# A two-layer attention encoder: the rotary table in a buffer of its own, the shared key moved ahead of the norms of the latents, and the modulation dot products moved behind it

## The chip, the cores and the metric

The kernel runs on one core of one Trainium2 chip. The time is the device time of one execution in microseconds (us); three executions of the kernel before were timed.

## What is computed

The model has two layers over 1024 tokens of width 1024. A vector `c` modulates each layer: `mod = silu(c) @ ada_w[i] + ada_b[i]` gives a shift, a scale and a gate of 1024 numbers each. Layer 0 mixes two kinds of attention, layer 1 is differential attention.

```python
c_act = jax.nn.silu(c)
for i in range(DEPTH):
    mod = c_act @ ada_w[i] + ada_b[i]
    shift, scale, gate = jnp.split(mod, 3, axis=-1)
    h = rms_norm(x, norm_g[i]) * (1.0 + scale[:, None, :]) + shift[:, None, :]
    ...
    x = x + gate[:, None, :] * out
...
# layer 0
cq, ckv, kr, q_sb, k_sb, v_sb, z = jnp.split(h @ w_in, cuts, axis=-1)
q = (rms_norm(cq, q_norm_g) @ w_uq).reshape(B, S, MLA_HEADS, MLA_NOPE + MLA_ROPE)
q = jnp.concatenate([q[..., :MLA_NOPE], rope(q[..., MLA_NOPE:], pos)], axis=-1)
kv = (rms_norm(ckv, kv_norm_g) @ w_ukv).reshape(B, S, MLA_HEADS, MLA_NOPE + MLA_V)
k_rope = jnp.broadcast_to(rope(kr[:, :, None, :], pos), (B, S, MLA_HEADS, MLA_ROPE))
```

What the change touches: `cq` and `ckv` are the latents, whose norms are needed as one number for each token; `kr` is the one rotated key that all heads share; `rope` needs a table of cosines and sines; `z` is a gate on the output of layer 0. The shift and scale of layer 1 and the two gates are not needed until much later in the program.

## The kernel before, in words

All tensors lie with 128 partitions. Every matrix product runs in three passes (high by high, low by high, high by low, `mm3`, lines 172 to 174) over 8 blocks of 128 inputs, so that a block of 128 outputs by 512 tokens, here called a half, is 24 matmuls. Weight blocks come by DMA into `w_st` (two buffers) and are split into `w_hi` (by ScalarE) and `w_lo` (by GpSimd, line 153). Results go to PSUM banks: three banks `sc`, two banks `psd`, two `tr`, one `pv`.

The stage that matters here ends the opening part, called `a0`, whose buffers are shared by tag (`ld` has six buffers of 1 MB, for weight loads `ada_st` and others; the tags `a` and `b` have four each). In program order it does this: the latents for both halves of the tokens; the rotary table `cs` (ten instructions of VectorE on `ar`, then a sine on ScalarE, line 637); `latent_norm` twice (row sums on the matmul engine at line 233, a reciprocal root on VectorE, a transpose at line 208, and `row_out`, which writes the row to DRAM); the norms read back on all partitions as `rqb`, and `te` and `to`, which combine them with the table and go to `tq_d`; the shared key's block (24 matmuls for each of two halves into `sc` banks, evacuated by VectorE at line 697, which multiplies by `cs`), its rotated copy (`krc`, line 718) and its store `krot_d`; and four `z` blocks of two halves each, evacuated by a sigmoid on ScalarE and a product on VectorE (line 250). Between them `more(n)` places pieces of `ada_rest`: 16 loads of 1 MB of modulation weights (`ada_st<-in_ada_r_dram`), each followed by two dot products with the vector `cb` on VectorE (line 522, `dots`). Then the first attention pair begins with its q/k block (`qk_k`, line 153, evacuated from `psd` banks), then its v block, again in `psd` banks.

A scheduler orders the instructions of each engine; each engine then runs its own in that order. SyncE (SP) issues all DMAs in one order, and each waits there for its buffer and its source. `tc.issue_after(x)` keeps an instruction behind `x` where both are on one engine, and nothing else.

The buffer of `cs` is tag `cs`, which has one buffer, and `cb` was put there first:

```python
cb = a0.tile([P, D], F32, name="cb", tag="cs")
...
cs = a0.tile([P, S], F32, name="cs", tag="cs")
```

So the table can't be written until the last dot product has read `cb`.

Of the kernel before, what the change touches and what calls it, by code (L numbers as in the profile page):

```python
# [11 lines left out]
F32 = mybir.dt.float32  # L12
# [4 lines left out]
ALU = mybir.AluOpType  # L17
# [4 lines left out]
P = 128  # L22
D = 1024
S = 1024
# [47 lines left out]
def kernel(ctx, tc, a, out):  # L72
    nc = tc.nc
    mm = nc.tensor.matmul

    def dma(dst, src):
        dst = dst.bitcast(F32) if dst.dtype == F32R else dst
        src = src.bitcast(F32) if src.dtype == F32R else src
        return nc.sync.dma_start(dst, src)
# [10 lines left out]
    def res(name, dt=F32R):  # L90

        return rpool.tile([P, S], dt, name=name, tag="res")
# [24 lines left out]
    krot_d = dram.tile([P, S], F32, name="krot_d")  # L117
# [37 lines left out]
    def split(hi, lo, src, eng_hi="act", eng_lo="vec"):  # L155

        if eng_hi == "act":
            nc.scalar.copy(hi, src)  # L158
        else:
            (nc.vector if eng_hi == "vec" else nc.gpsimd).tensor_copy(hi, src)  # L160
        return sub(eng_lo, lo, src, hi.bitcast(F32))

    def wprep(src, n=1024, eng_hi="act", eng_lo="pool", alloc=None):
        st = wpool.tile([P, 1024], F32, name="w_st", tag="w_st")
        dma(st[:, :n], src)
        alloc = alloc or (lambda name: wpool.tile([P, 1024], F32R, name=name, tag=name))
        hi, lo = alloc("w_hi"), alloc("w_lo")
        split(hi[:, :n], lo[:, :n], st[:, :n], eng_hi, eng_lo)
        return hi[:, :n], lo[:, :n]

    def mm3(ps, sh, sl, mh, ml, start, stop):
        mm(ps, sh, mh, start=start, stop=False)  # L172
        mm(ps, sh, ml, start=False, stop=False)  # L173
        mm(ps, sl, mh, start=False, stop=stop)  # L174

    def dense_fm(w, rhs, evac, bank=None):

        wh, wl = (t.rearrange("p (k c) -> p k c", c=P) for t in w)
        nk = len(rhs)
        for half in range(2):  # L180
            ps = (bank or d_bank)()
            sl = slice(half * 512, half * 512 + 512)
            for k in range(nk):
                mm3(ps, wh[:, k, :], wl[:, k, :], rhs[k][0][:, sl], rhs[k][1][:, sl], k == 0, k == nk - 1)
            evac(ps, half, sl)
# [290 lines left out]
    hT = [(res(f"h0h{k}"), res(f"h0l{k}")) for k in range(KC)]  # L476
    with tc.tile_pool(name="a0", bufs=1, reuse_waits="tile") as a0:
# [10 lines left out]
        def ada_load(k):  # L488
            ada_st[k] = a0.tile([P, 2, D], F32, name="ada_st", tag="ld", bufs=NLD)
            return dma(ada_st[k].rearrange("p i d -> p (i d)"), a["ada_t"][k - 1] if k else a["ada_0"])  # L490

        def wide(name, tag):
            return a0.tile([P, S], F32, name=name, tag=tag, bufs=4)
# [23 lines left out]
        def dots(st):  # L517

            m = a0.tile([P, 2], F32, name="adm", tag="adm", bufs=4)
            for n in range(2):  # L520
                junk = a0.tile([P, D], F32, name="junkd", tag="junkd")
                nc.vector.tensor_tensor_reduce(junk, st[:, n, :], cb, op0=ALU.mult, op1=ALU.add, scale=1.0, scalar=0.0,
                                               accum_out=m[:, n:n + 1])
            return m
# [8 lines left out]
        def x_mod(g, k, xts, lo):  # L533

            tr = t_bank()
            for j in range(4):
                nc.tensor.transpose(tr[:, j * P:(j + 1) * P], xts[j][:, k * P:(k + 1) * P], identf)
            hf = a0.tile([P, 512], F32, name="hf", tag="hf", bufs=3)
            sl = slice(g * 512, g * 512 + 512)
            nc.scalar.activation(hf, tr, AF.Identity, scale=gsc[0][:, k:k + 1], bias=modc[0][:, k:k + 1])  # L540
            hi = nc.scalar.copy(hT[k][0][:, sl], hf)
            return sub(lo, hT[k][1][:, sl], hf, hT[k][0][:, sl].bitcast(F32)), hi
# [38 lines left out]
        for k in range(KC):  # L581
            if k + 1 < KC:
                known = ada_block(k + 1)
                _, done = x_mod(0, k + 1, x0, "vec")
                if k + 4 < KC:
                    held = ada_load(k + 4)
# [22 lines left out]
        for k in range(KC):  # L609
            ready, _ = x_mod(1, k, x1, "vec")  # L610
# [8 lines left out]
        with tc.issue_after(ready.ins):  # L619

            pos_i = a0.tile([P, 1], I32, name="pos_i")
            dma(pos_i, a["pos"].to_broadcast([P, 1]))
            pos_f = a0.tile([P, 1], F32, name="pos_f")
            nc.vector.tensor_copy(pos_f, pos_i)
            ar = a0.tile([P, S], F32, name="ar", tag="ld", bufs=NLD)
            dma(ar, a["arange"].to_broadcast([P, S]))
            cs = a0.tile([P, S], F32, name="cs", tag="cs")
            nred = a0.tile([P, S], F32, name="nred", tag="junkd")
            nc.vector.tensor_scalar(ar, ar, pos_f, cst[:, 0:1], op0=ALU.add, op1=ALU.mult)
            nc.vector.tensor_scalar(nred, ar, 1.0 / (2.0 * math.pi), cst[:, 1:2], op0=ALU.mult, op1=ALU.add)  # L630
            nc.vector.tensor_scalar(nred, nred, 12582912.0, None, op0=ALU.add)
            nc.vector.tensor_scalar(nred, nred, -12582912.0, None, op0=ALU.add)
            for part in _two_pi_parts():
                nc.vector.scalar_tensor_tensor(ar, nred, -part, ar, op0=ALU.mult, op1=ALU.add)
            nc.vector.tensor_scalar(ar, ar, cst[:, 2:3], 3.1415925, op0=ALU.add, op1=ALU.min)
            nc.vector.tensor_scalar(ar, ar, -3.1415925, None, op0=ALU.max)
            nc.scalar.activation(cs, ar, AF.Sin, scale=cst[:, 3:4])


            lamt = a0.tile([P, 4, 64], F32, name="lamt", tag="ld", bufs=NLD)  # L640
            dma(lamt.rearrange("p n d -> p (n d)"), a["lam"].to_broadcast([P, 256]))
            lj = a0.tile([P, 2, 64], F32, name="lj")
            nc.vector.tensor_mul(lj, lamt[:, 0::2, :], lamt[:, 1::2, :])
            le = a0.tile([P, 2], F32, name="le")
            nc.vector.reduce_sum(le, lj, axis=AX.X)
            nc.scalar.activation(le, le, AF.Exp)
            nc.vector.tensor_tensor(neglam, le[:, 1:2], le[:, 0:1], op=ALU.subtract)
            nc.vector.tensor_scalar(neglam, neglam, -LAM_INIT, None, op0=ALU.add)
            nc.vector.tensor_scalar(subgl, subg, 0.5 * (1.0 - LAM_INIT), None, op0=ALU.mult)
# [17 lines left out]
        def ada_rest():  # L667
            bias = adab.rearrange("p (i n) -> p i n", n=8)
            for n in range(2):
                dst, b_ = ((gt, bias[:, 2::3, :]), (modc[1], bias[:, 3:5, :]))[n]  # L670
                dst = dst.rearrange("p (i n) -> p i n", n=8)
                for k in range(KC):
                    st = a0.tile([P, 2, D], F32, name="ada_st", tag="ld", bufs=NLD)
                    dma(st.rearrange("p i d -> p (i d)"), a["ada_r"][n, k])
                    nc.vector.tensor_tensor(dst[:, :, k], dots(st), b_[:, :, k], op=ALU.add)
                    yield k
        rest = ada_rest()

        def more(n):
            with tc.issue_after(ready.ins):  # L680
                for _ in range(n):
                    next(rest, None)

        def latent_norm(b0, n, row_d):
            part = lambda half, b: sqt[half, b // 2][:, b % 2 * 512:b % 2 * 512 + 512]
            for half in range(2):
                for b in range(b0 + 1, b0 + n):
                    nc.gpsimd.tensor_tensor(part(half, b0), part(half, b0), part(half, b), op=ALU.add)
            ss = row_sums(lambda t: part(t // 4, b0)[:, t % 4 * P:t % 4 * P + P], NT, v_bank)
            r = rstd_cols(a0, ss, NT, 1.0 / (n * P), 1e-6, "rl")  # L690
            row_out(a0, r, NT, row_d, v_bank)


        krt = wide("krt", "b")

        def kr_evac(ps, half, sl):
            nc.vector.tensor_mul(krt[:, sl], ps, cs[:, sl])
        latent_norm(0, 3, rq_d)
        latent_norm(3, 2, rkv_d)
        rqb = wide("rqb", "b")  # L700
        dma(rqb, row_bc(rq_d, P))
        more(3)
        te = wide("te", "a")
        nc.vector.tensor_copy(te[0:64], rqb[0:64])
        nc.vector.tensor_mul(te[64:128], rqb[64:128], cs[64:128])
# [2 lines left out]
        nc.vector.tensor_mul(to[0:64], rqb[0:64], cs[0:64])  # L708
        nc.vector.tensor_copy(to[64:128], rqb[64:128])
        dma(tq_d[1], to)  # L710
        with tc.issue_after(held.ins):
            wkr = wprep(a["w0"][21])
        dense_fm(wkr, hT, kr_evac, s_bank)
        more(2)
        krc = wide("krc", "b")
        for qd in range(4):
            o = qd ^ 1
            nc.scalar.copy(krc[32 * qd:32 * qd + 32], krt[32 * o:32 * o + 32])
        nc.gpsimd.tensor_tensor(krt, krt, krc, op=ALU.add)
        dma(krot_d, krt)  # L720
        more(2)

        for h in range(8):
            dma(rel_d[h], rel_r[h:h + 1, :].to_broadcast([24, NREL]))
# [214 lines left out]
    hT = [(res(f"h1h{k}"), res(f"h1l{k}")) for k in range(KC)]  # L939
# [302 lines left out]
```

## Time and profile before

| | |
|---|---|
| median of 3 runs | 1508.33 us (1505.69 to 1512.91) |
| the profiled execution's own time | 1512.19 us |
| its span | 1510.4 us |
| matmul engine (PE) busy | 1394.5 us, 92% |
| VectorE (DVE) busy | 937.2 us, 62% |
| ScalarE (ACT) busy | 679.3 us, 45% |
| GpSimd (POOL) busy | 421.6 us, 28% |

Times in the rows below are from the start of the span. Busy time of the matmul engine is modelled from pipelined starts, so its matmuls overlap: the distance between two starts is what one costs. An idle time in square brackets stands before an instruction, with what ended it.

### The profile page before, as it was taken

The numbers are of one execution on the slowest core, as the hardware profiler recorded it, in microseconds if no ns is written. First come the engines' busy times: TensorE is split into PE (matmuls) and PEld (weight loads), VectorE is DVE, ScalarE is ACT, GpSimd is POOL, SyncE is SP. The second block draws the span as 40 slices with busy tenths as digits, with TensorE's granted clock in tenths as the row PEclk, the third lists the DMA queues.
The fourth block names the chain that finished last, engine by engine and source line by source line (L and its number), as shares of the span: only waits on it lengthen the run. The fifth ranks groups of instructions, "written<-read, shape, count | busy, mean of one in ns | idle before, by whom it ended". The sixth has DMA issues, their size and how long they took to land.

```text
span 1510.4 us, 20851 instructions
## 1 busy us (share of the span) xinstructions
PE 1394.5 (92%) x7264; PEld 1163.6 (77%) x7264; DVE 937.2 (62%) x2137; ACT 679.3 (45%) x1380; POOL 421.6 (28%) x498
## 2 busy tenths in 40 slices
PE   5992999999998899999889899999999999998897
PEld 4771788888886678887667678888888888886686
DVE  5589127677778866576556616665565756557674
ACT  5630234565555654456444424444444535344321
POOL 2030221132325365535332221122221222133100
PEclk9995999999999899999989999999999999998899
DMA  9567331122315055543557132323232324336262
GB/s 373 216 235 308 117 114 50 49 82 58 94 32 221 29 182 176 166 130 102 178 164 242 48 98 63 84 85 105 77 98 63 91 63 114 79 104 179 79 197 95
DMA packets 110072, 190.38 MB, mean 126 GB/s; under 512 B 8784, under 2 KB 70088, under 8 KB 106896
## 3 DMA queue, kind: packets, MB, share of 16 engines
q1 hardware_dynamic: 109968, 189.05, 39.6%
q8 instruction: 58, 0.95, 0.3%
q14 instruction: 46, 0.38, 0.1%
HBM read 131.75 MB, written 39.27 MB: 113 GB/s over the span
## 4 chain that ended last, share of the span: by engine, by line
PE 39%; DMA 5%; DVE 4%; issue 2%; POOL 2%; ACT 1%; SPq 0%; DVEq 0%; POOLq 0%; ACTq 0%
PE psd L172 8%; PE psd L173 8%; PE psd L174 8%; PE sc L293 4%; PE pv L327 4%; PE sc L172 2%; PE sc L173 2%; PE sc L174 2%; DMA rb<-rst_d 1%; DMA qk_k<-qk_a 1%; DMA w_st<-in_wo_dram 1%; PE pv L233 1%; PE tr L309 1%; PE tr L307 1%; PE tr L308 1%
## 5 line engine op out<-in xcount | busy, mean ns | idle before, releaser
L153 POOL TENSOR_TENSOR w_lo<-w_st,w_hi 128x1024 fp32r<-128x1024 f32 (+2 forms) x61 | 145.1, 2381 | 348.3 <-ACT w_hi L158 348.0
L153 DVE TENSOR_TENSOR pt_l<-tr,pt_h 128x512 fp32r<-128x512 f32 (+1 forms) x240 | 148.9, 631 | 111.2 <-ACT pt_h L158 98.3
L158 ACT CAST pt_h<-tr 128x512 fp32r<-128x512 f32 (+1 forms) x240 | 126.1, 546 | 149.5 <-PE tr L309 141.6
L174 PE MATMUL psd<-h1h,w_lo 128*128 128x512 f32 x448 | 177.0, 395 | 0.0
L173 PE MATMUL psd<-h1l,w_hi 128*128 128x512 f32 x448 | 176.2, 393 | 0.0
L172 PE MATMUL psd<-h1h,w_hi 128*128 128x512 f32 x448 | 176.1, 393 | 0.0
L293 PE MATMUL sc<-qk_k,qk_a 128*128 128x512 f32 (+2 forms) x288 | 105.5, 371 | 5.1 <-DMA qk_a<-qk_a 2.8
L172 PE MATMUL psd<-h0h,w_hi 128*128 128x512 f32 x264 | 105.3, 399 | 0.0
L173 PE MATMUL psd<-h0l,w_hi 128*128 128x512 f32 x264 | 104.6, 396 | 0.0
L174 PE MATMUL psd<-h0h,w_lo 128*128 128x512 f32 x264 | 104.3, 395 | 0.0
L293 PE MATMUL sc<-qk_k,qk_b 128*128 128x512 f32 (+2 forms) x288 | 99.3, 351 | 0.0
L327 PE MATMUL pv<-pt_l,vt 128*128 128x256 f32 x320 | 91.3, 310 | 8.4 <-DVE pt_l L153 7.4
L1057 DVE CUSTOM_DVE_ANT_0 g<-sc,tz 128x512 f32<-128x512 f32 (+3 forms) x128 | 72.1, 585 | 40.8 <-PE sc L293 34.1
L173 PEld LDWEIGHTS psd<-h1l,w_hi 128*128 128x128 f32 x448 | 84.3, 188 | 16.9
L174 PEld LDWEIGHTS psd<-h1h,w_lo 128*128 128x128 f32 x448 | 84.2, 188 | 16.1
L172 PEld LDWEIGHTS psd<-h1h,w_hi 128*128 128x128 f32 x448 | 84.2, 188 | 16.1
L158 ACT CAST w_hi<-w_st 128x1024 fp32r<-128x1024 f32 x55 | 57.8, 1052 | 85.8 <-PE sc L173 39.7
L327 PE MATMUL pv<-pt_h,vt 128*128 128x256 f32 x320 | 91.6, 301 | 2.9 <-POOL pt_h L313 1.7
L1063 ACT ACTIVATE g<-g,st 128x640 f32<-128x640 f32 (+3 forms) x64 | 63.3, 990 | 67.4 <-DVE st L1062 62.5
L777 DVE TENSOR_TENSOR_SCAN g<-g 128x640 f32<-128x640 f32 (+3 forms) x32 | 68.8, 2149 | 14.7 <-ACT g L774 14.5
L327 PEld LDWEIGHTS pv<-pt_l,vt 128*128 128x128 f32 x320 | 64.1, 200 | 12.0 <-DVE pt_l L153 4.7
L327 PEld LDWEIGHTS pv<-pt_h,vt 128*128 128x128 f32 x320 | 63.7, 199 | 9.5 <-POOL pt_h L313 2.2
(458 smaller groups left out, 3722.9 us busy)
## 6 DMA issues: line engine op xcount, KB each, us to landing
w_st<-in_w_dram SPq DMA_DIRECT2D x43, 512.0 KB
ada_st<-in_ada_r_dram SPq DMA_DIRECT2D x16, 1024.0 KB
w_st<-in_wo_dram SPq DMA_DIRECT2D x16, 512.0 KB
ada_st<-in_ada_t_dram SPq DMA_DIRECT2D x7, 1024.0 KB
yh_d<-yh SPq DMA_DIRECT2D x28, 256.0 KB
yl_d<-yl SPq DMA_DIRECT2D x28, 256.0 KB
w_st<-in_wv_dram SPq DMA_DIRECT2D x12, 512.0 KB
qk_b<-qk_k SPq DMA_DIRECT2D x24, 256.0 KB
```

Of the source, the lines that this page charges most:

```text
L153: return (nc.vector if eng == "vec" else nc.gpsimd).tensor_tensor(out_, x_, y_, op=ALU.subtract)
L158: nc.scalar.copy(hi, src)
L172: mm(ps, sh, mh, start=start, stop=False)
L173: mm(ps, sh, ml, start=False, stop=False)
L174: mm(ps, sl, mh, start=False, stop=stop)
L233: mm(ps[:, t:t + 1], tile_of(t), ones, start=True, stop=True)
L293: mm(ps[:, :nn], st[:, q], mv[:, lo_:lo_ + nn], start=m == 0, stop=not diag and m == len(pairs) - 1)
L307: nc.tensor.transpose(tr[:, P:256], pb[:, (2 * j + 1) * P:(2 * j + 2) * P], identf)
L327: mm(dst, st, tt[w][:, m * 256:m * 256 + 256], start=j == 0 and m == 0 and x == 0, stop=j == n - 1 and m == 1 and x == len(ps_) - 1)
L777: nc.vector.tensor_tensor_scan(ur, ur, ur, 1.0, op0=ALU.mult, op1=ALU.bypass)
L1057: nc.vector.tensor_tensor_reduce(e_[:, sl], ps, tz[:, S - L + sl.start:S - L + sl.stop], op0=ALU.add, op1=ALU.max, scale=1.0, scalar=-3e38 ...
L1063: nc.scalar.activation(e_[:, :L], e_[:, :L], AF.Exp, scale=0.125, bias=st[:, 2 + c:3 + c], accum_out=lst[:, c1:c1 + 1] if c == 0 else st[: ...
```

## The change

The rotary table gets one of the four buffers of tag `b` (and `krt` one of tag `a`), so that it no longer waits for `cb`. The shared key's block comes ahead of the norms of the latents. Of the 16 weight loads of `ada_rest` two stay early, and 14 must be issued behind the store of the rotated key (`turned`); the calls of `more` that stood between the norms and the key are gone.

```diff
-            cs = a0.tile([P, S], F32, name="cs", tag="cs")
+            cs = wide("cs", "b")
...
                 for k in range(KC):
                     st = a0.tile([P, 2, D], F32, name="ada_st", tag="ld", bufs=NLD)
-                    dma(st.rearrange("p i d -> p (i d)"), a["ada_r"][n, k])
-                    nc.vector.tensor_tensor(dst[:, :, k], dots(st), b_[:, :, k], op=ALU.add)
+                    with tc.issue_after((turned if n or k > 1 else held).ins):
+                        dma(st.rearrange("p i d -> p (i d)"), a["ada_r"][n, k])
+                    with tc.issue_after(turned.ins):
+                        nc.vector.tensor_tensor(dst[:, :, k], dots(st), b_[:, :, k], op=ALU.add)
                     yield k
...
         def more(n):
-            with tc.issue_after(ready.ins):
-                for _ in range(n):
-                    next(rest, None)
+            for _ in range(n):
+                next(rest, None)
...
-        krt = wide("krt", "b")
+        krt = wide("krt", "a")
...
+        with tc.issue_after(held.ins):
+            wkr = wprep(a["w0"][21])
+        dense_fm(wkr, hT, kr_evac, s_bank)
         latent_norm(0, 3, rq_d)
         latent_norm(3, 2, rkv_d)
         rqb = wide("rqb", "b")
         dma(rqb, row_bc(rq_d, P))
-        more(3)
...
-        with tc.issue_after(held.ins):
-            wkr = wprep(a["w0"][21])
-        dense_fm(wkr, hT, kr_evac, s_bank)
-        more(2)
...
-        dma(krot_d, krt)
-        more(2)
+        turned = dma(krot_d, krt)
+        more(4)
```

On VectorE, at the key's evacuation (`krt<-sc,cs`, which frees two of the three `sc` banks), the kernel before has this order:

```order
L675 TENSOR_TENSOR modc_121<-adm,smalls 128x2
L522 ISA junkd,adm<-ada_st,cb 128x1024
L522 ISA adm 128x1
L522 ISA junkd,adm<-ada_st,cb 128x1024
L522 ISA adm 128x1
L704 COPY te<-rqb 64x1024
L709 COPY to<-rqb 64x1024
L675 TENSOR_TENSOR modc_121<-adm,smalls 128x2
L705 TENSOR_TENSOR te<-rqb,cs 64x1024
L708 TENSOR_TENSOR to<-rqb,cs 64x1024
L697 TENSOR_TENSOR krt<-sc,cs 128x512 x2
```

The same engine in the changed kernel, at the same evacuation (`lat_l` is the last of the latents, `gt` the gates' column, `rlh` the first step of the norms' root):

```order
L522 ISA junkd,adm<-ada_st,cb 128x1024
L522 ISA adm 128x1
L522 ISA junkd,adm<-ada_st,cb 128x1024
L522 ISA adm 128x1
L605 SCALAR_TENSOR_TENSOR lat_l<-sc,smalls,lat_h 128x512
L677 TENSOR_TENSOR gt<-adm,smalls 128x2
L698 TENSOR_TENSOR krt<-sc,cs 128x512 x2
L191 TENSOR_SCALAR rlh<-pv 128x8
```

The evacuation of the key stood behind the dot products of all 16 loads; now it stands behind those of two, and ahead of the norms, of `te` and of `to`.

Further on VectorE, at the evacuation of the first q/k block (`qk_k<-psd,qk_a`), before:

```order
L697 TENSOR_TENSOR krt<-sc,cs 128x512 x2
L242 TENSOR_SCALAR gsc_123<-modc_121 128x8
L250 TENSOR_TENSOR zb<-zb,sc 128x512
L243 TENSOR_TENSOR gsc_123<-gsc_123,smalls 128x8
L250 TENSOR_TENSOR zb<-zb,sc 128x512 x7
L153 TENSOR_TENSOR qk_k<-psd,qk_a 128x512 x2
```

and in the changed kernel, at the same place:

```order
L677 TENSOR_TENSOR modc_121<-adm,smalls 128x2
L522 ISA junkd,adm<-ada_st,cb 128x1024
L522 ISA adm 128x1
L522 ISA junkd,adm<-ada_st,cb 128x1024
L522 ISA adm 128x1
L677 TENSOR_TENSOR modc_121<-adm,smalls 128x2
L242 TENSOR_SCALAR gsc_123<-modc_121 128x8
L243 TENSOR_TENSOR gsc_123<-gsc_123,smalls 128x8
L153 TENSOR_TENSOR qk_k<-psd,qk_a 128x512 x2
```

Before, only products of `z` blocks stood ahead of it; now the dot products of all the weight loads do.

On the queue of SyncE, behind the row of norms (`rq_d`) and ahead of the first attention's weights, the changed kernel has:

```order
L79 DMA rq_d<-row 8x128
L79 DMA rqb<-rq_d 128x1024
L79 DMA tq_d<-te 128x1024
L79 DMA tq_d<-to 128x1024
L79 DMA krot_d<-krt 128x1024
L79 DMA ada_st<-in_ada_r_dram 128x2048 x2
L79 DMA zs_d<-zb 128x1024
L79 DMA ada_st<-in_ada_r_dram 128x2048 x4
L79 DMA w_st<-in_w_dram 128x1024
L79 DMA ada_st<-in_ada_r_dram 128x2048
L79 DMA rkv_d<-row 8x128
L79 DMA zs_d<-zb 128x1024
```

Before, all 16 `ada_st` loads stood ahead of `rqb`, and `krot_d` followed `tq_d` in the same way. The other seven now follow in the same manner, between two more stores of `z` and three more weight blocks.

## Rows read from the trace of the kernel before

**Rows 1.** The page: busy tenths of the matmul engine in 40 slices of 37.8 us.

```profile
PE   5992999999998899999889899999999999998897
```

**Rows 2.** Waits of the matmul engine, 98 to 220 us: total, times, longest.

```profile
PE sc L172 <- DVE krt L697: 17.9, 1, 17.9
```

**Rows 3.** Timeline of the matmul engine: start, duration, instruction, [idle before <- releaser].

```profile
98.70 0.50 PE L172 MATMUL sc<-h0h,w_hi 128*128 128x512 f32 x1
...
100.66 0.95 PE L233 MATMUL pv<-ones_sq,lsq 128*128 128x1 f32 x8
...
116.83 0.39 PE L174 MATMUL sc<-h0h,w_lo 128*128 128x512 f32 x1
...
153.11 0.80 PE L172 MATMUL sc<-h0h,w_hi 128*128 128x512 f32 x1 [17.90 <-DVE krt L697]
...
154.13 0.63 PE L174 MATMUL sc<-h0h,w_lo 128*128 128x512 f32 x1
154.56 0.63 PE L172 MATMUL sc<-h0h,w_hi 128*128 128x512 f32 x1
...
159.15 0.39 PE L173 MATMUL sc<-h0l,w_hi 128*128 128x512 f32 x1
159.38 0.39 PE L174 MATMUL sc<-h0h,w_lo 128*128 128x512 f32 x1
...
215.37 0.60 PE L268 MATMUL tr<-identf,vs 128*128 128x128 f32 x4
```

**Rows 4.** Timeline of ScalarE: the rotary table, and the swapped copy of the key.

```profile
148.47 1.15 ACT L637 ACTIVATE cs<-ar,smalls 128x1024 f32<-128x1024 f32 x1 [34.48 <-DVE adm L522]
...
153.74 4.20 ACT L718 COPY krc<-krt 32x1024 f32<-32x1024 f32 x4 [2.21 <-DVE gsc L242]
```

**Rows 5.** Timeline of VectorE: dot products, and one instruction that reads PSUM.

```profile
92.08 0.74 DVE L605 SCALAR_TENSOR_TENSOR lat_l<-psd,smalls,lat_h 128x512 fp32r<-128x512 f32 x1
...
104.30 0.16 DVE L675 TENSOR_TENSOR gt<-adm,smalls 128x2 f32<-128x2 f32 x1
...
111.49 1.23 DVE L522 CUSTOM_DVE_ANT_0 junkd<-ada_st,cb 128x1024 f32<-128x1024 f32 x1
...
112.83 3.44 DVE L522 CUSTOM_DVE_ANT_0 junkd<-ada_st,cb 128x1024 f32<-128x1024 f32 x1
...
138.13 1.22 DVE L522 CUSTOM_DVE_ANT_0 junkd<-ada_st,cb 128x1024 f32<-128x1024 f32 x1
...
140.73 1.22 DVE L522 CUSTOM_DVE_ANT_0 junkd<-ada_st,cb 128x1024 f32<-128x1024 f32 x1
```

**Rows 6.** Windows: busy time of each engine, granted clock, DMA share, GB/s.

```profile
110.00:115.00 5.00, 5.00 (x23) 4.13 (x22) 5.00 (x12) 2.34 (x2) 2.23 (x1) 1.00 1.04 436
135.00:140.00 5.00, 0.22 (x1) 0.00 (x0) 4.68 (x10) 0.00 (x0) 0.00 (x0) 0.50 1.01 419
```

**Rows 7.** Queue of SyncE and GpSimd: a row of norms out to DRAM and back.

```profile
988.89 0.30 SPq L79 DMA_DIRECT2D rst_d<-row  x1
...
993.60 1.29 POOL L1089 TENSOR_TENSOR zt<-zt,rb 128x512 f32<-128x512 f32 x1 [2.94 <-DMA rb<-rst_d]
```

**Rows 8.** VectorE by line and form, 98 to 220 us: count, busy, mean ns, idle.

```profile
L250 DVE TENSOR_TENSOR zb<-zb,sc 128x512 f32<-128x512 f32 x8 | 5.5, 687 | 36.7 <-ACT zb L248 36.7
...
L708 DVE TENSOR_TENSOR to<-rqb,cs 64x1024 f32<-64x1024 f32 x1 | 1.2, 1218 | 0.0
...
L709 DVE COPY to<-rqb 64x1024 f32<-64x1024 f32 x1 | 0.7, 691 | 0.0
```

**Rows 9.** Timeline of GpSimd: the low halves of weight blocks.

```profile
87.83 6.59 POOL L153 TENSOR_TENSOR w_lo<-w_st,w_hi 128x1024 fp32r<-128x1024 f32 x2 [22.42 <-ACT w_hi L158]
...
112.77 2.42 POOL L153 TENSOR_TENSOR w_lo<-w_st,w_hi 128x1024 fp32r<-128x1024 f32 x1 [12.74 <-ACT w_hi L158]
```

**Rows 10.** Queue of SyncE: the first and last of the q/k copies.

```profile
206.83 0.54 SPq L79 DMA_DIRECT2D qk_b<-qk_k  x1
...
213.31 0.47 SPq L79 DMA_DIRECT2D qk_a<-qk_a  x1
```

## The prediction

> **What bounds the kernel now.** I read the page first: the matmul engine is busy for 92% of the span, and after the first slice its strip falls to 2 in one place only, the slice from 113 to 151 us [rows 1], so that one hole is worth a look of its own. The waits of that engine in this stretch come next: the longest, 17.9 us, is on the key's evacuation by VectorE [rows 2], and small instructions of the norms break up the rest of the hole. The timeline of the matmul engine gives the hole its edges: the last matmul of the first `z` half starts at 116.83, the first of the second half at 153.11 [rows 3]. The reader is to see that the second is of the same block as the first, and that only a bank was missing. Three `sc` banks exist; two held the two halves of the key, the third the first half of `z`. ScalarE's timeline says why the key was not evacuated: it stood idle for 34 us before the sine that makes `cs`, released by a dot product of VectorE [rows 4]. `cs` shares its one buffer with `cb`, which every dot product reads. So the hole is a buffer's, not an engine's: the matmul engine waits for the table, the table for the last of 16 weight loads of 1 MB.
>
> Inside the hole VectorE and the DMA engines both work without a pause: a pair of dot products takes 2.60 us from start to start (138.13 to 140.73) [rows 5], and the DMA share is full at 419 GB/s [rows 6]. That work isn't removed by the change. It moves, and the question is what it meets.
>
> **The change part by part.**
>
> *Removed.* In the changed order the key is evacuated behind the dots of two loads. Before, these were done at 104.3 [rows 5], and the sine needs none of them now; the key's two halves end at about 105 and 111 (48 matmuls from 98.70 [rows 3]). So the bank for the second half of the first `z` block is free before it is asked for, and the hole closes: 153.11 less 117.06 (the last start plus one step of 0.23) is 36.0 us. Behind the hole the first 12 matmuls also ran at the lower level of the clock, 1.2 GHz, 0.43 us apart where the later ones are 0.23 apart [rows 3]; the granted clock in the hole is 0.50 [rows 6]: 12 x 0.20 = 2.4 us more. Together 38.4.
>
> *Added on the matmul engine's path.* The row sums of the second latent and three transposes ran inside the hole and now stand between matmuls: 16 rows of line 233 at 0.95 us for 8 [rows 3], 1.9, and three transposes at 0.3 (four take 0.60 in the last of [rows 3], so this estimate is generous), 0.9; 2.8 in all. The moved key block costs what it cost. Net 35.6 us. Before, the v block ends at 215.37, and its 48 matmuls take 10.9 (48 x 0.227 [rows 3]), so the first q/k block ended at 204.5. By this sum it ends at 168.9.
>
> *Where the dots go.* The loads may start only behind the store of the key, and that stands on SyncE behind a chain, which I follow in time. The transpose of the norms is 8 matmuls into the second `z` half, 118.9; its copy and the issue of `rq_d`, 119.5. Out to DRAM and back on all partitions took 4.7 us for a row of half the width (988.89 to 993.60 [rows 7]); with 0.6 for the other half 124.8. `te` and `to` are two copies at 0.69 and two products at 1.22 [rows 8], 3.8, done at 128.6. The key's own part (its copy on ScalarE, 4.20 [rows 4], and GpSimd's sum of 2.4, taken as one such instruction [rows 9]) is over by 118.5 (111 + 0.7 + 4.2 + 2.4) and doesn't count. So the key's store issues at 129.0, and the first of 14 loads at 129.3. Ahead of it in the DMA engines are `te`, `to` and the key, 0.52 MB each; from 127.1, with about 1.2 us to start (an estimate from the 4.7 us of two such trips and their 0.26 MB [rows 7]) and 2.6 MB at 0.425 MB/us (between the two rates of [rows 6]), the first load is there at 134.5, say 135.
>
> From there two bounds. *DMA*: 14 loads of 1.05 MB, four `z` stores and four weight blocks of 0.52 MB that stand between them, and the three stores ahead: 20.45 MB, 48.1 us from 128.3, so the last load lands at 176.4 and its dots end at 179.0. *VectorE*: 14 x 2.60 = 36.4; five evacuations of `z` halves that lie between at 0.69 [rows 8], 3.4; two rows of norms and gates, 0.6; and what GpSimd takes. One dot product that began beside a GpSimd split took 3.44 us instead of 1.23, the split 2.42 [rows 5, 9]: 2.2 lost. Four splits fall into this stretch (the last `z` block, two q/k, one v), 8.8. That ends at 184.2. An evacuation that reads PSUM kept its 0.74 in the middle of two such splits [rows 5, 9], so I charge nothing for those.
>
> The Trainium skill, page "SBUF — State Buffer", section "SBUF: two separate sides", says that GpSimd and a VectorE instruction with two SBUF inputs take one shared port pair as an exclusive lock for a whole instruction, the loser fully blocked. By that rule a split costs its full 2.4, four 9.6, and VectorE would end at 185.0; without any such lock it would end at 175.4 and the DMA bound of 179.0 would hold. The row agrees with the rule.
>
> I take VectorE's bound, since the row of 3.44 is this same pair of instructions, and keep 179.0 for the low end. Two small instructions and one evacuation (0.3 + 0.7) later the first q/k half is out of its bank: 185.2, or 180.0.
>
> *The new wait.* The first q/k evacuation now stands behind all dots on VectorE. The v block needs that `psd` bank. The `z` halves themselves don't wait. Each needs the evacuation of the third half back. With 5.45 us a half from 117.1 and the additions above, the matmul engine asks for one at 130 that stands behind `te` and `to` (out at 129.3), and at 147 and 152 for two that stand behind one and two loads (out at 138 and 144). So the matmul engine runs to 168.9 and stands until 185.2: 16.3, plus 2.4 for the low clock again, 18.7. Behind the v block stand the three copies of q and k, issued over 6.5 us before (206.83 to 213.31 [rows 10]), so about 195 against an end of v at 198.5: hidden, with 3 us to spare.
>
> *The other edits.* `krt` in tag `a` and `cs` in tag `b` take buffers whose last readers, the transposes of `x` and the sums of squares, stand ahead of the key's block; nothing. The later gates and modulation are wanted hundreds of us later; nothing. The scheduler also interleaves the following attention differently; the matmul engine is full there, so I give it 0 and 4 us either way.
>
> **Sum.** 35.6 - 18.7 = 16.9 us. Span 1510.4 to 1493.5, the profiled execution's own time 1512.19 to 1495.3; that execution is 3.9 above the median, so the median goes from 1508.33 to 1491.4. Half a per cent, 7.5 us, is about what a measurement here can tell from no change.
>
> **The rivals.**
>
> *A shorter stall.* The DMA bound decides, or the chain to the key's store is quicker. At 180.0 the stall is 11.1 + 2.4 and the gain 22.1: 1486. If the dots end by 168.9 there is none: 35.6, 1473. For it: GpSimd's two splits at 87.83 took 6.59 where two alone take 4.8 [rows 9], so some of the loss may fall on GpSimd, which has time. Against the last: 20.45 MB from 128.3 to 166 would need 540 GB/s, against 436 in [rows 6].
>
> *A longer stall.* Each us by which the store of the key or the stream is late is a us lost. At four fifths of the rate that I took the stream needs 60 us and the last dots end at 191, a gain of 10: 1498; with the store of the key 4 us late too, 195, a gain of 6: 1502. The stores of `z` and the row of norms make such delays possible, since SyncE waits at each. The Trainium skill, "DMA: Bandwidth & Descriptors", section "Where 436 GB/s comes from", holds HBM to about 358 GB/s for one core, by which I estimate 57.1 us for the stream, dots until 188.0 and 1495; the 419 and 436 of [rows 6] contradict it.
>
> *Slower than before.* The queue of SyncE becomes a ring: a load behind a `z` store, the store behind an evacuation, that behind the dots of the load before. If each load ran alone, 1.2 + 2.5 + 2.6 = 6.3 us, 14 end at 217, the v block starts 15 us later than before: 1523. The point that decides is 5.2 us for each load, (202.1 - 129.3) / 14. Against it: six buffers, and six loads issued with one store between them.
>
> *It doesn't do what it says*: `cs` waits for another reader in tag `b`. Then the hole stays, 1508. The earlier tile in that buffer is an `x` tile, long read, so little speaks for it.
>
> **How the numbers follow.** Forecast (1486 to 1498) 0.60; shorter stall (1473 to 1486) 0.22; longer (1498 to 1507) 0.12; slower 0.03; unchanged 0.03. The likeliest is 1491.4. The range 1475 to 1499 holds the forecast, most of the shorter stall and a little of the longer. Faster by over 0.5% (under 1500.8): 0.60 + 0.22 + 0.04 = 0.86. Slower 0.03. Within: 0.11.
>
> **What would show it.** Right: no wait for `krt` in the matmul engine; the sine at about 102; the first late load issued at 129; the `z` blocks without a gap; one wait of 11 to 19 us before the v block, on `qk_k`; dot products of 3.4 us beside splits. Wrong: waits inside the `z` blocks, the DMA share below full between 130 and 175, a start of the loads far from 129, or scores that wait for the copies of q and k.

## The result and the profile after

The changed kernel takes 1493.59 us (median of 4 runs, 1491.70 to 1493.87). The kernel before, with a fourth run, takes 1508.99 us (median, 1505.69 to 1512.91). The ratio is 0.9894, 95% interval 0.9869 to 0.9920: 15.4 us faster. The profiled execution took 1493.56 us, its span is 1491.8 us against 1510.4. The forecast was 1491.4 us.

The page, busy time of the matmul engine and its strip in 40 slices (now of 37.3 us), answers to [rows 1]:

```profile
PE 1386.7 (93%) x7264; PEld 1155.6 (77%) x7264; DVE 950.9 (64%) x2137; ACT 679.3 (46%) x1380; POOL 428.3 (29%) x498
...
PE   5999599999998799998879899999999999997797
```

The slice that read 2 is gone, and the next one reads 5: it runs from 149 to 186 us. The waits of the matmul engine from 98 to 220 us (total, times, longest) answer to [rows 2]:

```profile
PE psd L172 <- DVE qk_k L153: 15.6, 1, 15.6
PE sc L172 <- DVE zb L250: 0.7, 1, 0.7
```

The wait for the key is no longer there, and one new wait has come, for the first q/k evacuation. The timeline of the matmul engine answers to [rows 3]:

```profile
130.24 0.50 PE L172 MATMUL sc<-h0h,w_hi 128*128 128x512 f32 x1 [0.75 <-DVE zb L250]
...
184.56 0.80 PE L172 MATMUL psd<-h0h,w_hi 128*128 128x512 f32 x1 [15.65 <-DVE qk_k L153]
...
198.37 0.60 PE L268 MATMUL tr<-identf,vs 128*128 128x128 f32 x4
...
198.72 0.47 PE L293 MATMUL sc<-qk_k,qk_a 128*128 128x512 f32 x1
```

The reader is to see three things. The `z` half that asks for a bank at 130 loses only 0.75 us. The first q/k block is done at 168.91 (184.56 less 15.65). The scores start right behind the v block, with no wait for the copies of q and k. The transpose of v stands at 198.37; it stood at 215.37 in [rows 3], so the stage ends 17.0 us earlier; 0.57 of these were gained ahead of it (the key's block starts at 98.13, at 98.70 in [rows 3]). The other 1.6 us of the span's 18.6 lie somewhere behind the stage; no run looks for them.

ScalarE has the sine of the table at 101.01, where [rows 4] had it at 148.47:

```profile
101.01 1.16 ACT L637 ACTIVATE cs<-ar,smalls 128x1024 f32<-128x1024 f32 x1
```

VectorE's timeline answers to [rows 5]: the key's second half, the copy of `te`, the first late dot product, two dot products and two small instructions that met a GpSimd split, the first dot product of the last load, and the q/k evacuation.

```profile
110.33 0.69 DVE L698 TENSOR_TENSOR krt<-sc,cs 128x512 f32<-128x512 f32 x1 [5.30 <-PE sc L174]
...
123.98 2.11 DVE L707 COPY te<-rqb 64x1024 f32<-64x1024 f32 x1 [5.09 <-DMA rqb<-rq_d]
...
136.60 1.23 DVE L522 CUSTOM_DVE_ANT_0 junkd<-ada_st,cb 128x1024 f32<-128x1024 f32 x1 [3.24 <-DMA ada_st<-in_ada_r_dram]
...
137.87 3.29 DVE L522 CUSTOM_DVE_ANT_0 junkd<-ada_st,cb 128x1024 f32<-128x1024 f32 x1
...
155.20 2.81 DVE L522 CUSTOM_DVE_ANT_0 junkd<-ada_st,cb 128x1024 f32<-128x1024 f32 x1
...
161.35 1.55 DVE L677 TENSOR_TENSOR modc<-adm,smalls 128x2 f32<-128x2 f32 x1
...
175.77 2.17 DVE L677 TENSOR_TENSOR modc<-adm,smalls 128x2 f32<-128x2 f32 x1
...
180.80 1.23 DVE L522 CUSTOM_DVE_ANT_0 junkd<-ada_st,cb 128x1024 f32<-128x1024 f32 x1 [0.25 <-DMA ada_st<-in_ada_r_dram]
...
183.82 1.28 DVE L153 TENSOR_TENSOR qk_k<-psd,qk_a 128x512 fp32r<-128x512 f32 x2
```

From 136.60 to 183.82 VectorE has no idle time but 0.25 us, and these are for the last load: both bounds of the prediction end at the same place. GpSimd's splits, one beside `te` and the first and last of that stretch, answer to [rows 9], the windows (busy time of each engine, clock, DMA share, GB/s) to [rows 6]:

```profile
123.19 2.35 POOL L153 TENSOR_TENSOR w_lo<-w_st,w_hi 128x1024 fp32r<-128x1024 f32 x1 [5.28 <-ACT w_hi L158]
136.96 3.12 POOL L153 TENSOR_TENSOR w_lo<-w_st,w_hi 128x1024 fp32r<-128x1024 f32 x1 [11.42 <-ACT w_hi L158]
...
174.55 3.37 POOL L153 TENSOR_TENSOR w_lo<-w_st,w_hi 128x1024 fp32r<-128x1024 f32 x1 [11.67 <-ACT w_hi L158]
```

```profile
128.00:130.00 2.00, 1.50 (x7) 0.92 (x5) 1.93 (x4) 0.00 (x0) 0.00 (x0) 1.00 0.63 262
...
130.00:140.00 10.00, 9.76 (x43) 7.99 (x44) 6.45 (x18) 2.14 (x3) 3.04 (x1) 1.00 0.99 349
140.00:150.00 10.00, 10.00 (x45) 8.27 (x45) 9.83 (x19) 1.20 (x2) 0.08 (x1) 1.00 1.02 431
...
170.00:180.00 10.00, 0.00 (x0) 0.00 (x0) 9.79 (x16) 2.02 (x3) 5.21 (x3) 0.67 1.00 397
180.00:190.00 10.00, 5.44 (x13) 4.33 (x14) 4.68 (x12) 0.00 (x0) 0.21 (x4) 0.50 0.53 161
```

From 130 to 180 us the DMA engines are as full as VectorE. The queue of SyncE has the key's store, the first late loads and the copies of q and k ([rows 10] had the first and the last at 206.83 and 213.31):

```profile
129.71 0.38 SPq L79 DMA_DIRECT2D krot_d<-krt  x1
130.15 2.02 SPq L79 DMA_DIRECT2D ada_st<-in_ada_r_dram  x2
...
185.16 0.54 SPq L79 DMA_DIRECT2D qk_b<-qk_k  x1
...
193.61 0.46 SPq L79 DMA_DIRECT2D qk_a<-qk_a  x1
```

### The profile page after: what moved, and what is told of

Read it like the earlier page. It is cut to its first block, busy times and chain, and to the rows that moved or that the text cites. A ratio compares the mean times of both kernels' runs of the same rounds, so it can differ in the third digit from the quotient of the medians.

```text
span 1491.8 us, 20861 instructions
## 1 busy us (share of the span) xinstructions
PE 1386.7 (93%) x7264; PEld 1155.6 (77%) x7264; DVE 950.9 (64%) x2137; ACT 679.3 (46%) x1380; POOL 428.3 (29%) x498
## 4 chain that ended last, share of the span: by engine, by line
PE 39%; DMA 6%; DVE 4%; issue 2%; POOL 2%; ACT 1%; SPq 0%; DVEq 0%; POOLq 0%; ACTq 0%
PE psd L172 7%; PE psd L173 7%; PE psd L174 7%; PE sc L293 4%; PE pv L327 4%; PE sc L172 2%; PE sc L173 2%; PE sc L174 2%; DMA rb<-rst_d 1%; DMA qk_k<-qk_a 1%; DMA w_st<-in_wo_dram 1%; PE pv L233 1%; DMA y_hi<-yh_d 1%; PE tr L307 1%; PE tr L309 1%
## 5 line engine op out<-in xcount | busy, mean ns | idle before, releaser
L153 POOL TENSOR_TENSOR w_lo<-w_st,w_hi 128x1024 fp32r<-128x1024 f32 (+2 forms) x61 | 149.5, 2453 | 369.4 <-ACT w_hi L158 365.5
L172 PE MATMUL psd<-h0h,w_hi 128*128 128x512 f32 x264 | 106.6, 404 | 15.6 <-DVE qk_k L153 15.6
L173 PEld LDWEIGHTS psd<-h1l,w_hi 128*128 128x128 f32 x448 | 84.2, 188 | 16.9
L776 DVE TENSOR_TENSOR_SCAN g<-g 128x640 f32<-128x640 f32 (+3 forms) x32 | 65.8, 2056 | 20.4 <-ACT g L773 20.4
L172 PEld LDWEIGHTS psd<-h0h,w_hi 128*128 128x128 f32 x264 | 50.5, 191 | 25.6 <-DVE qk_k L153 16.1
```

The source lines that it names most:

```text
L153: return (nc.vector if eng == "vec" else nc.gpsimd).tensor_tensor(out_, x_, y_, op=ALU.subtract)
L776: nc.vector.tensor_tensor_scan(ur, ur, ur, 1.0, op0=ALU.mult, op1=ALU.bypass)
```

## The experiments

The theory is that of the prediction: VectorE has 36 us of dot products to do between the norms and the first attention; whoever stands behind them on VectorE waits. The buffer alone doesn't change that, the order does. Rivals: the buffer was the whole hole; the late start of the loads is the whole stall; the DMA stream alone, or VectorE alone, sets its end. Each kernel was timed beside the kernel before on one chip, and ratios are to it.

### The parts of the change

**e1_buffer_alone**: the kernel before with one line.

```diff
-            cs = a0.tile([P, S], F32, name="cs", tag="cs")
+            cs = wide("cs", "b")
```

> The kernel before with one line of the change: the rotary table in a buffer of its own; everything else as before. The theory (the buffer lets the table be early, but where the dot products stand in VectorE's order decides when the banks are freed): the sine moves from 148 to before 110, yet in the order of this kernel the key's evacuation stands behind the dots of about 12 loads and the z products behind those of all 16 and te and to, so the matmul engine still waits about 20 us for the key's evacuation and again for the first z product; the gain is 11 to 14 us, a median of 1495 to 1498. The rival (the buffer was the whole hole, the move of the key and of the loads adds nothing): no wait over 3 us before the z blocks, no wait at the v block either, a gain of about 33 us, 1475.

Measured: 1502.98 us, ratio 0.9962 (0.9947 to 0.9977); span 1500.0. Its waits of the matmul engine, 95 to 222 us:

```profile
PE pv L208 <- DVE rlr L202: 7.8, 2, 6.5
PE sc L172 <- DVE krt L697: 5.3, 1, 5.3
PE sc L172 <- DVE zb L250: 4.9, 1, 4.9
PE pv L233 <- DVE row L210: 3.6, 1, 3.6
```

```profile
137.25 1.28 DVE L697 TENSOR_TENSOR krt<-sc,cs 128x512 f32<-128x512 f32 x2
```

The sine runs at 101.17, yet the key's evacuation only at 137.25, behind the dots of about twelve loads. The rival falls: the buffer alone brings 0.4%. The theory was right on the place and wrong by 5 us on the size: the hole breaks into five waits of 21.6 us together, and I had left out that the small steps of the norms (L202, L210) stand between the dots as well.

**e2_loads_not_held**: the changed kernel, with the late loads free to start early.

```diff
-                    with tc.issue_after((turned if n or k > 1 else held).ins):
+                    with tc.issue_after(held.ins):
```

> The changed kernel, with the 14 late loads free to start as early as the two early ones (not held behind the store of the key). The theory (VectorE has 36 us of dots to do somewhere; held behind the key they meet the v block, not held they meet the z blocks): the z products stand behind all dots on VectorE, the hole comes back at the second z half (about 128 to 151 us), the wait of 15.6 us at the v block goes; 1494 to 1497. The rival (only the late start of the loads costs, earlier loads take the stall away): no wait over 5 us anywhere from 98 to 220, 1475.

Measured: 1504.11 us, 0.9969 (0.9955 to 0.9983). Its waits, 98 to 222 us:

```profile
PE sc L172 <- DVE zb L250: 12.5, 1, 12.5
PE pv L208 <- DVE modc L677: 9.9, 2, 5.7
PE pv L233 <- DVE row L210: 1.6, 1, 1.6
```

The stall at the v block is gone, and 24.0 us of waits stand around the norms and the `z` blocks instead. So most of the gain of the change (10.5 of its 15.4 us by the medians) hangs on holding the loads back, and the rival, that earlier loads would only help, falls. No run holds the loads and leaves the key where it was, so what the key's move adds to the held loads is not shown. The size was missed by 7 us: the dots end at 152.7, `te` and `to` follow, and the second `z` half starts at 157.9 where I had 151.

**e3_loads_behind_read_back** and **e9_early_loads_norms_first**: the changed kernel, the loads held behind the read-back of the norms, 8 us earlier; in e9 the dots also stand behind the second norm's root on VectorE.

```diff
-                    with tc.issue_after((turned if n or k > 1 else held).ins):
+                    with tc.issue_after((back if n or k > 1 else held).ins):
...
-        dma(rqb, row_bc(rq_d, P))
+        back = dma(rqb, row_bc(rq_d, P))
```

```diff
-                    with tc.issue_after(turned.ins):
+                    with tc.issue_after((normed if n or k > 1 else held).ins):
```

> The changed kernel, with the late loads held behind the read-back of the norms (rqb) and not behind the store of the key: the first six loads are issued about 9 us earlier, ahead of the stores of te, to and the key. The theory (the start of the stream sets the end of the dots, both bounds shift with it): the last dots end 6 to 9 us earlier, the wait of 15.6 us at the v block falls to 7 to 10, new waits in the z blocks of at most 3; 1485 to 1489. The rival (VectorE's queue or the copies of q and k behind the v block set the end, the start of the stream does not): the wait stays at 13 to 16 or is replaced in full, 1492 to 1495.

> The changed kernel with the late loads held behind the read-back only, as in e3_loads_behind_read_back, but with the dot products kept behind the reciprocal root of the second norm on VectorE, where they had been mixed into it. The theory (after the norms VectorE alone needs 46 to 47 us for the dots and what lies among them, wherever the stream starts): no wait at the second norm's transpose, the first late dot at 133 to 134 instead of 136.6, the evacuation of the first q/k block at 179 to 182 instead of 183.9, the waits of the matmul engine in the stage 12 to 16 in all; 1488 to 1492. The rival (the start of the DMA stream sets the end, which is 8 us earlier here): the evacuation at 175 to 177, 1484 to 1487.

Measured: e3 1499.83 us, 0.9934 (0.9911 to 0.9957); e9 1494.32 us, 0.9929 (0.9905 to 0.9953). Waits of e3 and VectorE's one long idle time in it:

```profile
PE psd L172 <- DVE qk_k L153: 6.8, 1, 6.8
PE pv L208 <- DVE rlr L202: 5.9, 1, 5.9
PE sc L172 <- DVE zb L250: 2.1, 2, 1.3
```

```profile
160.01 0.69 DVE L250 TENSOR_TENSOR zb<-zb,sc 128x512 f32<-128x512 f32 x1 [5.83 <-ACT zb L248]
```

Waits of e9:

```profile
PE sc L172 <- DVE zb L252: 7.6, 2, 6.9
PE psd L172 <- DVE qk_k L153: 6.8, 1, 6.8
```

The wait at the v block fell to 6.8, about as expected of e3, but the time did not follow. The dots start at 131.5 and 134.0 instead of 136.6, and the first q/k evacuation still comes at 186.5 and 186.2 (183.82 in the changed kernel, whose stage starts 1.2 to 1.4 us sooner). With the loads early, their dots fill VectorE while the `z` blocks run: the matmul engine waits for a bank, then the next sigmoid is late, and VectorE, whose next instruction needs it, stands idle for 5.83 us (3.97 in e9). In e9 14.4 us of waits are left, as expected, in two places instead of one. Two holes also cost the slower start twice: in e3 twelve steps of the matmul engine behind the first (150.37 to 155.66) and thirteen behind the second (187.24 to 192.95) take 0.44 us each, where the changed kernel has thirteen such steps in all. My 1485 to 1489 for e3 was wrong by 11 us. In e9 the theory's time was 2 us too early (6 by the ratio, since the kernel before took 1505.25 there) and its evacuation 4; from its first dot to that evacuation VectorE needed 52.2 us and not 46 to 47. The rival's evacuation was 9 us too early: an earlier stream buys nothing here.

### What sets the length of the stall

**e6_no_mod1_loads**: eight of the 14 late loads and their dots left out.

```diff
+                if n == 1:
+                    nc.vector.tensor_copy(dst, b_)
+                    return
```

> The changed kernel without the 8 loads and 16 dot products of layer 1's shift and scale, which are replaced by their bias (that part of the modulation is left out). The theory: the dots that are left end by about 157 us, before the first q/k block is done at 169; the wait of 15.6 us at the v block and the low clock behind it (2.4) go, at most 3 us of them coming back as a wait for the copies of q and k; 1473 to 1479. The rival (the stall is caused by something else that stands in front of the evacuation): a wait of over 8 us stays there, 1485 or more.

Measured: 1472.66 us, 0.9757 (0.9738 to 0.9776). These waits are left:

```profile
PE sc L293 <- DMA qk_a<-qk_a: 0.9, 1, 0.9
PE sc L172 <- DVE zb L250: 0.8, 1, 0.8
```

The stall comes from these loads and their dots together; this run takes both away and can't say which. The time falls by 20.9 us (1493.59 less 1472.66; ratios 0.9894 less 0.9757 give 20.7). In the trace, from the start of the key's block (99.56) to the transpose of v (181.25), the stage is 18.6 us shorter than in the changed kernel (98.13 to 198.37), which is the stall and its slower start as counted, 15.65 and 2.8. The other 2.3 us lie outside the stage or in the spread of the runs.

**e4_half_dots** and **e5_half_bytes** take half off one bound and leave the other.

```diff
+                        m = dots(st) if n == 0 and k < 2 else dots(st, (0,))
```

```diff
+                            dma(st[:, 0, :], a["ada_r"][n, k][:, 0:D])
```

> The changed kernel with one of the two dot products of each late load (the other half of the modulation behind the key's store is left out), all bytes still loaded. The theory (two bounds of nearly one length, the DMA stream and VectorE, so taking off one gains little): the stream still runs at 0.42 MB/us, the last load lands at 176 to 179, the wait at the v block falls from 15.6 to 9 to 13; 1488 to 1492. The rival (VectorE alone set the end): the dots end near 165, no wait over 3 us at the v block, 1473 to 1478.

> The changed kernel with half the bytes in each of the 14 late loads, both dot products reading that half (half of the weights behind the key's store are left out). The theory (VectorE's own work is 14 x 2.60 for the dots, 3.4 for the z products, 0.6 for rows and about 7 lost to GpSimd's splits, 47.4 in all): first dot at 133 to 135, the dots end at 180.5 to 182.5, the wait at the v block is 13 to 15; 1490 to 1493. The rival (the DMA stream alone set the end): 13 MB are there by 163, the wait falls under 4, 1473 to 1480.

Measured: e4 1488.31 us, 0.9882 (0.9854 to 0.9910); e5 1491.40 us, 0.9894 (0.9870 to 0.9918). In e4, the wait of the matmul engine and the last load's dot on VectorE:

```profile
PE psd L172 <- DVE qk_k L153: 14.5, 1, 14.5
```

```profile
180.84 1.23 DVE L522 CUSTOM_DVE_ANT_0 junkd<-ada_st,cb 128x1024 f32<-128x1024 f32 x1 [2.54 <-DMA ada_st<-in_ada_r_dram]
```

In e5, the wait, the first late dot, and the window of 160 to 170 us:

```profile
PE psd L172 <- DVE qk_k L153: 15.4, 1, 15.4
```

```profile
138.95 3.01 DVE L522 CUSTOM_DVE_ANT_0 junkd<-ada_st,cb 128x1024 f32<-128x1024 f32 x1 [4.05 <-DMA ada_st<-in_ada_r_dram]
```

```profile
160.00:170.00 10.00, 9.70 (x44) 8.06 (x45) 9.86 (x19) 0.82 (x2) 3.23 (x1) 1.00 0.76 270
```

Both rivals fall. With half the dots VectorE waits for the DMA at 12 of the 14 loads, and the last load is there at 180.84, as in the changed kernel (180.80): the stream alone takes that long. With half the bytes the DMA engines have room (share 0.76) and VectorE has none: from its first dot to the q/k evacuation it takes 47.2 us (138.95 to 186.16), as in the changed kernel (136.60 to 183.82). Two bounds of one length: halving either takes 0.2 to 1.2 us off the wait of 15.6, and two traces of the changed kernel alone differ by 0.8 (16.4 in **after_beside_e8** below). The times came out as expected, the places did not quite: in e4 the last load was to land by 179 and the wait to fall to 9 to 13; in e5, whose stage begins 1.5 us later, the first dot was due by 135 and the end of the last by 182.5 (it ends at 185.7). Both sums took a stream that starts at full rate; in e5 even a first load of half the bytes was not there sooner (7.3 us after its issue, 6.4 in the changed kernel).

### A version without the new wait

**e7_qk_off_vector** lets ScalarE copy the first q/k block out and GpSimd subtract; **e8_qk_off_vector_ordered** also keeps the next block's split behind that on both engines, and the next `z` weights behind the copies of q and k on SyncE. From the edit of e8:

```diff
+            if tmp is not None:
+                nc.scalar.copy(tmp[:, sl], ps)
+                hi = nc.scalar.copy(a_t[:, sl], tmp[:, sl])
+                copied[:] = [hi, sub("pool", k_t[:, sl], tmp[:, sl], a_t[:, sl].bitcast(F32))]
...
+                with tc.issue_after(copied[0].ins), tc.issue_after(copied[1].ins):
+                    w_next = wprep(a["w0"][2 * pr + 1])
...
+    with tc.issue_after(copied[2].ins):
+        dma(rkv, row_bc(rkv_d, P))
```

> The changed kernel; the first q/k block alone is copied out of its banks by ScalarE and split there and on GpSimd, so that its evacuation no longer stands behind the dots on VectorE; the copies of q and k go ahead of two loads for later on SyncE. Nothing is left out. The theory (the wait at the v block is nothing but the place of that evacuation behind the dots): no wait on the q/k evacuation, the v block starts at about 169; a new wait of 4 to 8 us behind it, since the attention's buffers lie where the loads lay and are free when the dots end, at about 186 with two more GpSimd splits beside them; 1480 to 1487. The rival (the whole wait comes back at the attention's buffers or at the copies of q and k): 1490 to 1495.

> The kernel of e7_qk_off_vector, where ScalarE's copy of the first q/k block stood behind the split of the second q/k block's weights (which waited for its DMA until 174), and GpSimd's subtraction behind that split too. Here the split of those weights is kept behind the q/k block on both engines, and the weights of the z block of the first pair behind the copies of q and k on SyncE. Nothing is left out. The theory (with the evacuation behind nothing but its own block the v block needs no wait; what is left is the copies of q and k beside the stream, and the end of the dots): the wait of 6.0 us at the v block goes, the first copy issues at 172 to 175 and not at 184, the scores start at 186 to 190 (193.16 in that kernel, 198.72 in the changed one); 1481 to 1485. The rival (the scores wait for VectorE and the DMA stream all the same, so an earlier v block is given back): scores at 192 or later, 1486 to 1489.

Measured: e7 1487.90 us, 0.9863 (0.9840 to 0.9886); e8 1482.89 us, 0.9848 (0.9826 to 0.9871). In e7, the waits, and ScalarE at the copy:

```profile
PE psd L172 <- ACT zt L369: 6.0, 1, 6.0
PE sc L293 <- DMA qk_a<-qk_a: 3.1, 1, 3.1
```

```profile
173.97 1.04 ACT L158 CAST w_hi<-w_st 128x1024 fp32r<-128x1024 f32 x1 [13.88 <-DMA w_st<-in_w_dram]
174.92 1.06 ACT L369 COPY zt<-psd 128x512 f32<-128x512 f32 x2
```

The time is 0.9 us above what I gave. The new wait has the expected length, but not from the place that I gave. It is the same fault in small: the copy stood on ScalarE behind a split that waited 13.88 us for the next block's weights, in the DMA stream. In e8 that wait is gone; its waits are these, and the scores start at 186.83 (198.72 in the changed kernel):

```profile
PE psd L174 <- POOL w_lo L153: 3.1, 1, 3.1
PE sc L293 <- DMA qk_a<-qk_a: 1.9, 1, 1.9
```

```profile
186.83 0.79 PE L293 MATMUL sc<-qk_k,qk_a 128*128 128x512 f32 x1 [1.86 <-DMA qk_a<-qk_a]
```

Changed kernel and e8 were then run side by side, as **after_beside_e8** and **e8_beside_after**.

> The changed kernel once more, unchanged, on the same chip as e8_beside_after, so that the two can be compared without a difference of chips: 1.0 to 1.3 per cent under the kernel before.

> The kernel of e8_qk_off_vector_ordered, unchanged. If its shorter stage (scores at 186.83 and not at 198.72) reaches the end of the program, it is 8 to 12 us faster than the changed kernel beside it; the rival, that the time is given back later, has it within 4 us.

Measured: 1492.53 us, 0.9898 (0.9881 to 0.9915), and 1483.79 us, 0.9828 (0.9804 to 0.9853). e8 is 8.7 us faster than the change and leaves nothing out: the wait at the v block was the place of one evacuation behind other work, and of the 11.9 us by which the scores start sooner most are kept to the end.

## Why the prediction was right

*What bounds it, and the hole.* Right, but for one reading: VectorE and the DMA engines did not work without a pause inside the hole. VectorE stands idle for 2.32 us before 126.04, and the DMA share is 0.45 from 128 to 132 us and nothing from 146 to 148, where the last load has landed and dots are still to do. That changes no term of the sum. The matmul engine waits no longer for the key, and the first q/k block ends at 168.91 where 168.9 was predicted. It does so from a start 0.57 us earlier, so the stage itself took that much longer than the sum has it.

*The change needs its parts together.* The prediction took the hole away as one piece, by the buffer and the order. e1 and e2 show that the buffer does not do it without the held loads: alone it brings 6.0 us, with the new order 4.9. Whether the held loads need the moved key is not shown.

*The chain to the store of the key.* Nearly right: `rq_d` at 118.92 (119.5), the row back at 123.98 (124.8), the first late load at 130.15 (129.3). The copy of `te` took 2.11 us, not 0.69, beside a split of GpSimd at 123.19.

*VectorE's bound.* Right in kind, and in part lucky in its end: 184.2 predicted for the end of the dots, 183.3 found. The first dot came 1.6 us late (136.60 for 135), and the work was 2.5 us shorter (46.7 for 49.2); the two misses nearly cancel. The four GpSimd splits cost VectorE about 7.0 us (2.1 and 1.6 on dot products, 1.4 and 2.0 on instructions of 128x2 that else take 0.16), not 8.8. The reason is one that the prediction gave to a rival: part of the loss falls on GpSimd, whose splits took 2.78 to 3.37 instead of 2.4. At 136.96 the split starts inside a dot product; the next dot product, 137.87, ends at 141.16, 1.08 us after the split's end at 140.08. The Trainium skill, "SBUF — State Buffer", section "SBUF: two separate sides", describes the port pair that the two engines share as an exclusive lock, held for a whole instruction while the other is blocked; these rows agree, for either engine as the loser.

*The DMA bound.* This term was mis-sized: the last load was to land at 176.4 and did at 180.80. Of these 4.4 us 2.6 are the start: from 128 to 140 the stream moved 4.0 MB (262 GB/s to 130, 349 behind it), which at the 425 of the sum takes 9.4 us and not 12. The last ten us, at 397, are part of the rest. The rate of the sum came from two windows in the middle of a stream; the trace of the kernel before had a slower one at a full share:

```profile
102.00:110.00 8.00, 8.00 (x34) 5.83 (x33) 7.93 (x18) 0.48 (x1) 0.00 (x0) 1.00 0.98 317
```

What holds the rate there no run shows. The three stores ahead of the loads are not enough of a reason: in e3 they are issued at 128.71 to 131.09 into a running stream, which does not slow down (share 1.01, 420 GB/s, and 421 from 140 to 170):

```profile
126.00:140.00 14.00, 13.25 (x60) 10.71 (x60) 13.64 (x25) 1.92 (x3) 2.57 (x2) 1.00 1.01 420
```

The other rates agree with [rows 6] (419 to 431). The 358 GB/s of the Trainium skill, "DMA: Bandwidth & Descriptors", section "Where 436 GB/s comes from", are again passed. That the sum held is luck here: VectorE stood idle only 0.25 us for the last load, since the real end of the stream fell on the point to which its own work had come. The low end of the range for a quicker VectorE, 1486, was therefore not to be had, as e4's wait of 14.5 shows.

*The new wait.* Right: 15.65 us where 16.3 were predicted, and 2.8 where 2.4 for the slower start: at a granted clock of 0.50, the lower level of 1.2 GHz, to which it fell while the matmul engine stood still (0.67 in the mean of 170 to 180), the fourteen matmuls from 184.56 to 190.27 go 0.44 us apart. The v block ended at 198.37 (198.5), with the copies of q and k hidden behind it.

*The rival of a longer stall.* "Each us by which the store of the key or the stream is late is a us lost" does not hold the other way round: 8 us earlier gained nothing (e3, e9). The rival for a slower kernel was a ring through SyncE; none is seen there, and the DMA share stays at 0.99 to 1.02 from 130 to 180. A ring of another kind appears in e3 and e9, in VectorE's own order: the matmul engine waits for VectorE, and VectorE for a sigmoid behind the matmul engine. With the slower start paid twice it ate the gain of the early loads, without making the kernel slower than before.

*The sum.* 16.9 us predicted; 17.0 at the end of v, 18.6 of the span and 15.4 of the medians found. The profiled execution of before was slower than its median by 3.2 us, that of after was at its median, which is the difference of the last two.

## What to carry to other kernels

A wait that is read off a buffer may be held up by an order as well: freeing the buffer moved the sine by 47 us and the key's evacuation by 15. Work that VectorE must do somewhere has to be placed where nobody behind it is needed soon, or the urgent instruction has to go to another engine; moving its loads earlier only chose who waits (e2, e3, e9). Placing them later still, behind the first q/k evacuation, was not run. When two streams of one length feed each other, halve each alone before believing that one is the bound. A rate read in the middle of a stream is not the rate of its start.

## What the runs showed of the hardware

In the changed kernel, instructions of 128x2 and 128x8 elements, 0.15 to 0.17 us alone, took 1.55 to 2.39 us when they met a GpSimd split or addition (161.35 and 175.77 above; 2.37 at 111.32, 2.39 at 115.54). They lost 1.4 to 2.2 us, as much as a dot product of 128x1024 (1.6 and 2.1). A full DMA share did not mean full bytes: 349 GB/s at 0.99 against 431 at 1.02, ten us later.
